# Averaging 8,192 rows in windows of 16: each partition owns 64 neighbouring rows, and the output stays on chip until the last load

## The chip, the cores and the metric

The kernel runs on one core of a Trainium2 chip. The metric is device time in microseconds (us), taken as the median of several runs; less is better. A timed run is the whole program. A separately profiled execution gives the trace that the views below come from, and its span (first to last instruction) is a little shorter than a timed run.

## What is computed

The input `x` is float32 of shape (32, 256, 4096) and `output_size` is 256. Length 4096 splits evenly, so every output is the mean of 16 neighbouring values:

```python
for i in range(output_size):
    start = int(i * length / output_size)
    end = int((i + 1) * length / output_size)
    result[:, :, i] = np.mean(x[:, :, start:end], axis=-1)
```

Batch and channel are only a list of 8,192 rows of 4096 values (16 KB each). A core reads 134.2 MB, writes 8.4 MB, and does one addition per value read.

## The kernel before, in words

**Tiling.** The 8,192 rows are cut into 16 tiles of 512 rows, 8.4 MB each. A tile is a contiguous piece of DRAM: partition p of tile t holds the R = 4 rows 512t + 4p to 512t + 4p + 3. So a partition's share of a tile is 64 KB without a gap, and the shares of neighbouring partitions are 64 KB apart in DRAM (`x3`). In the output the same four rows are 4 KB, and neighbouring partitions are 4 KB apart (`out3`).

**Buffers.** `inpool` has two input tiles `xin` of 64 KB per partition; `foldpool` two fold buffers of 8 KB; `accpool` three sums of 4 KB; `outpool` three results of 4 KB; `defer_buf` holds four tiles' results (16 KB) until the end. A tile framework puts in the semaphore waits: load t + 2 goes into the buffer of tile t, so its issue on the queue of SyncE (SP) waits until the readers of tile t are done.

**One steady tile** (`steady_plan`). One load of 8.4 MB on the SP queue (line 152). Of the tile's 1,024 windows, VectorE (DVE) sums the first 512 directly over 16 values (`vdir`, line 168). For the other 512, GpSimd (POOL) first adds the two halves of each window, 8 + 8 values, into a fold buffer, in two pieces of 256 windows (`fold`, line 161); VectorE then sums the remaining 8 values (`vfold`, line 177). ScalarE (ACT) multiplies by 1/16 (`mulA`, line 184) and issues the tile's store of 512 KB on its own queue (`store`, line 200).

**Exceptions.** The first two tiles' loads are each split over the SP and ACT queues (`ramp`). Tiles 9 to 12 (`DEFER`) aren't stored when done: their results wait in `defer_buf`. Tiles 13 and 14 (`two_chunk_plan`) are loaded in two halves. The last tile (`last_plan`) is loaded in six pieces, from 4,096 KB down to 256 KB; behind them in the SP queue stands one store of the four deferred tiles (`dstore_all`, line 194, 2,048 KB); its results go out in two stores of 896 and 128 columns, each split over both queues (lines 206 and 209).

**What sets the order.** Each engine and each queue works in program order. Transfers that one queue has issued are worked off one after another by the core's 16 DMA engines; transfers of the SP and the ACT queue share these engines. There is no planner.

Of the kernel before, what the change touches and what calls it, by code (L numbers as in the profile page):

```python
# [9 lines left out]
def kernel(  # L10
# [5 lines left out]
):  # L16
    nc = tc.nc

# [5 lines left out]
    hw = window // 2  # L24

    rows = batch * channels
    P = nc.NUM_PARTITIONS

    R = 4
    IN_BUFS = 2  # L30
    RAMP_TILES = 2

    assert rows % (P * R) == 0
    ntiles = rows // (P * R)

    x3 = x.rearrange("b c l -> (b c) l").rearrange(
        "(t p r) l -> t p (r l)", p=P, r=R
    )
    out3 = out.rearrange("b c o -> (b c) o").rearrange(
        "(t p r) o -> t p (r o)", p=P, r=R  # L40
    )

    inv_w = 1.0 / float(window)
    groups = R * output_size
    cols = R * length
    half_g = groups // 2
    quarter_g = groups // 4
    FOLD_CAP = 256
    DEFER_N = 4
    DEFER_T0 = ntiles - 3 - DEFER_N  # L50
    DEFER = set(range(DEFER_T0, DEFER_T0 + DEFER_N))

    out_def = out.rearrange("b c o -> (b c) o").rearrange(
        "(t p r) o -> p t (r o)", p=P, r=R
    )

    inpool = ctx.enter_context(tc.tile_pool(name="inpool", bufs=IN_BUFS))
    foldpool = ctx.enter_context(tc.tile_pool(name="foldpool", bufs=2))
    accpool = ctx.enter_context(tc.tile_pool(name="accpool", bufs=3))
    OUT_BUFS = 3  # L60
    outpool = ctx.enter_context(tc.tile_pool(name="outpool", bufs=OUT_BUFS))
    deferpool = ctx.enter_context(tc.tile_pool(name="deferpool", bufs=1))
    defer_buf = deferpool.tile([P, DEFER_N * groups], mybir.dt.float32)
    defer3 = defer_buf.rearrange("p (t o) -> p t o", t=DEFER_N, o=groups)

    def steady_plan(i, ramp=False):
        ops = []
        if ramp:
            ops.append(("load", 0, cols // 2, "sync"))
            ops.append(("load", cols // 2, cols, "scalar"))  # L70
        else:
            ops.append(("load", 0, cols, "sync"))
        ops += [
            ("fold", half_g, half_g + quarter_g),
            ("fold", half_g + quarter_g, groups),
            ("vdir", 0, half_g),
            ("vfold", half_g, half_g + quarter_g),
            ("vfold", half_g + quarter_g, groups),
            ("mulA", 0, groups),
        ]  # L80
        if i not in DEFER:
            ops.append(("store", 0, groups))
        return ops

    def two_chunk_plan(i):
        h = cols // 2
        ops = [
            ("load", 0, h, "sync"),
            ("load", h, cols, "sync"),
        ]  # L90
        for c in range(2):
            g0 = c * half_g
            ops.append(("fold", g0 + 192, g0 + 352))
            ops.append(("fold", g0 + 352, g0 + 512))
            ops.append(("vdir", g0, g0 + 192))
            ops.append(("vfold", g0 + 192, g0 + 352))
            ops.append(("vfold", g0 + 352, g0 + 512))
        ops += [
            ("mulA", 0, groups),
            ("store", 0, groups),  # L100
        ]
        return ops

    def last_plan(i):
        sizes = [256, 256, 192, 128, 64, 64, 32, 32]
        assert sum(sizes) == groups
        bounds = [0]
        for s in sizes:
            bounds.append(bounds[-1] + s)
        ops = []  # L110
        load_bounds = [0, 512, 832, 896, 960, 992, 1024]
        for k in range(len(load_bounds) - 1):
            g0, g1 = load_bounds[k], load_bounds[k + 1]
            ops.append(("load", g0 * window, g1 * window, "sync"))
        ops.append(("dstore_all",))
        part1 = 896
        for k, s in enumerate(sizes):
            g0, g1 = bounds[k], bounds[k + 1]
            if s >= 128:
                m = (g0 + g1) // 2  # L120
                ops.append(("fold", m, g1))
                ops.append(("vdir", g0, m))
                ops.append(("vfold", m, g1))
            else:
                ops.append(("vdir", g0, g1))
            if g1 == part1:
                ops.append(("mulA", 0, part1))
                ops.append(("store2", 0, part1))
        ops.append(("mulV", part1, groups))
        ops.append(("store2", part1, groups))  # L130
        return ops

    def plan_for(i):
        if i < RAMP_TILES:
            return steady_plan(i, ramp=True)
        idx_from_end = ntiles - 1 - i
        if idx_from_end == 0:
            return last_plan(i)
        if idx_from_end <= 2:
            return two_chunk_plan(i)  # L140
        return steady_plan(i)

    def emit(i, ops, bufs):
        xin, xin_2d, acc, res = bufs
        fold_tiles = {}

        for op in ops:
            kind = op[0]
            if kind == "load":
                _, c0, c1, qname = op  # L150
                q = nc.sync if qname == "sync" else nc.scalar
                q.dma_start(out=xin_2d[:, c0:c1], in_=x3[i][:, c0:c1])  # L152
            elif kind == "fold":
                _, g0, g1 = op
                n = g1 - g0
                assert n <= FOLD_CAP
                ftile = foldpool.tile(
                    [P, FOLD_CAP, hw], mybir.dt.float32, name="foldt"
                )
                fold_tiles[(g0, g1)] = ftile  # L160
                nc.gpsimd.tensor_add(  # L161
                    out=ftile[:, 0:n, :],
                    in0=xin[:, g0:g1, 0:hw],
                    in1=xin[:, g0:g1, hw:window],
                )
            elif kind == "vdir":
                _, g0, g1 = op
                nc.vector.reduce_sum(  # L168
                    out=acc[:, g0:g1],
                    in_=xin[:, g0:g1, :],  # L170
                    axis=mybir.AxisListType.X,
                )
            elif kind == "vfold":
                _, g0, g1 = op
                ftile = fold_tiles[(g0, g1)]
                n = g1 - g0
                nc.vector.reduce_sum(  # L177
                    out=acc[:, g0:g1],
                    in_=ftile[:, 0:n, :],
                    axis=mybir.AxisListType.X,  # L180
                )
            elif kind == "mulA":
                _, g0, g1 = op
                nc.scalar.mul(out=res[:, g0:g1], in_=acc[:, g0:g1], mul=inv_w)  # L184
            elif kind == "mulV":
                _, g0, g1 = op
                nc.vector.tensor_single_scalar(  # L187
                    out=res[:, g0:g1],
                    in_=acc[:, g0:g1],
                    scalar=inv_w,  # L190
                    op=mybir.AluOpType.mult,
                )
            elif kind == "dstore_all":
                nc.sync.dma_start(
                    out=out_def[:, DEFER_T0 : DEFER_T0 + DEFER_N, :],
                    in_=defer3[:, 0:DEFER_N, :],
                )
            elif kind == "store":
                _, g0, g1 = op
                nc.scalar.dma_start(  # L200
                    out=out3[i][:, g0:g1], in_=res[:, g0:g1]
                )
            elif kind == "store2":
                _, g0, g1 = op
                h = P // 2
                nc.scalar.dma_start(
                    out=out3[i][h:P, g0:g1], in_=res[h:P, g0:g1]
                )
                nc.sync.dma_start(
                    out=out3[i][0:h, g0:g1], in_=res[0:h, g0:g1]  # L210
                )
            else:
                raise AssertionError(kind)

    res_by_tile = {}

    def new_bufs(i):
        xin = inpool.tile([P, groups, window], mybir.dt.float32)
        xin_2d = xin.rearrange("p o w -> p (o w)")
        acc = accpool.tile([P, groups], mybir.dt.float32)  # L220
        if i in DEFER:
            j = i - DEFER_T0
            res = defer_buf[:, j * groups : (j + 1) * groups]
        else:
            res = outpool.tile([P, groups], mybir.dt.float32)
        res_by_tile[i] = res
        return xin, xin_2d, acc, res

    ramp_bufs = []
# [49 lines left out]
```

## Time and profile before

| | |
|---|---|
| Timed runs (3) | 337.47 us median (337.29 to 337.67) |
| Span of the profiled execution | 335.2 us |
| Part of a timed run outside the span | 337.47 - 335.2 = 2.3 us |
| VectorE busy | 209.5 us (62%) in 64 instructions |
| GpSimd busy | 145.6 us (43%) in 42 instructions |
| ScalarE busy | 18.1 us (5%) in 17 instructions |
| DMA | 142.62 MB in 6033 packets, mean 425 GB/s over the span |

The profiled execution has no separate time of its own beside its span, so the row "outside the span" sets the span against the median of the timed runs.

How to read the views: the page gives each engine's busy time as a digit (tenths) in 40 equal slices of the span, and below that the mean busy share of the 16 DMA engines and the GB/s they moved. The chain of waits follows the work that ended last backwards to what released it. The timeline lists instructions in order, with the idle time before each and what ended it. The table of windows gives busy time per engine, DMA share and GB/s for stretches of the span. The trace also has a record of every single DMA packet with its size and duration; a packet is one contiguous run between DRAM and one partition, moved by one of the 16 engines.

### The profile page before, as it was taken

How to read it: one execution, taken by the hardware profiler on the slowest of the kernel's cores; microseconds unless marked ns; L12 is line 12 of the kernel's file. 1: busy time of each engine (PE TensorE's matmuls, PEld its weight loads, DVE VectorE, ACT ScalarE, POOL GpSimd, SP SyncE). 2: the span in 40 equal slices, each digit the busy share in tenths (PEclk: the TensorE clock that was granted, in tenths of full speed). 3: DMA queues.
4: the chain of work that ended last, by engine and by line, in shares of the span. 5: the costliest groups of instructions: out<-in, count | busy, mean ns of one | idle time of the engine just before them, and what ended most of it. 6: DMA issues, size and time to landing. Idle time of an engine off the chain costs nothing.

```text
span 335.2 us, 279 instructions
## 1 busy us (share of the span) xinstructions
DVE 209.5 (62%) x64; ACT 18.1 (5%) x17; POOL 145.6 (43%) x42
## 2 busy tenths in 40 slices
DVE  0029295590956919478293773928659299765595
ACT  1000101001010000101001010010100101000101
POOL 0027091550906419063280723708154276664460
DMA  8999999999999999999999999999898999999997
GB/s 317 434 438 438 501 399 399 475 456 399 399 476 455 399 399 493 438 399 399 516 414 399 399 532 399 399 400 507 375 501 375 438 438 438 438 396 458 404 410 273
DMA packets 6033, 142.62 MB, mean 425 GB/s; under 512 B 656, under 2 KB 784, under 8 KB 3344
## 3 DMA queue, kind: packets, MB, share of 16 engines
q1 hardware_dynamic: 4000, 128.19, 89.0%
q10 hardware_dynamic: 2032, 14.42, 10.2%
q14 instruction: 1, 0.01, 0.0%
HBM read 134.22 MB, written 8.39 MB: 425 GB/s over the span
## 4 chain that ended last, share of the span: by engine, by line
DMA 78%; POOL 18%; DVE 2%; issue 0%; SPq 0%; ACTq 0%; POOLq 0%
DMA xin<-in_x_dram 78%; POOL foldt L161 18%; DVE acc L168 1%; DVE acc L177 0%; SPq L152 0%; ACTq L152 0%; DVE res L187 0%; POOLq L161 0%
## 5 line engine op out<-in xcount | busy, mean ns | idle before, releaser
L161 POOL TENSOR_TENSOR foldt<-xin 128x2048 f32<-128x2048 f32 (+4 forms) x38 | 145.4, 3848 | 180.4 <-DMA xin<-in_x_dram 178.4
L168 DVE TENSOR_REDUCE acc<-xin 128x512 f32<-128x8192 f32 (+5 forms) x25 | 137.4, 5504 | 118.6 <-DMA xin<-in_x_dram 118.6
L177 DVE TENSOR_REDUCE acc<-foldt 128x256 f32<-128x2048 f32 (+4 forms) x38 | 73.9, 1976 | 3.3 <-POOL foldt L161 3.1
L184 ACT ACTIVATE res<-acc 128x1024 f32<-128x1024 f32 (+1 forms) x12 | 12.6, 1047 | 234.6 <-DVE acc L177 220.4
L184 ACT ACTIVATE defer_buf<-acc 128x1024 f32<-128x1024 f32 x4 | 4.2, 1056 | 75.6 <-DVE acc L177 75.6
L184 ACT ACT_TABLE_LOAD x1 | 1.3, 1283 | 1.7 <-PEq L260 1.7
L187 DVE TENSOR_SCALAR res<-acc 128x128 f32<-128x128 f32 x1 | 0.2, 226 | 0.0
L260 POOL MEMSET const-float32-0.0<- 128x1 f32 x1 | 0.1, 98 | 0.2 <-issue 0.2
L260 POOL MEMSET const-bfloat16-1.0<- 128x1 bf16 x1 | 0.1, 102 | 0.0
L260 POOL MEMSET const-uint8-127<- 128x1 uint8 x1 | 0.1, 102 | 0.0
L260 POOL MEMSET const-float32-1.0<- 128x1 f32 x1 | 0.1, 98 | 0.0
## 6 DMA issues: line engine op xcount, KB each, us to landing
xin<-in_x_dram SPq DMA_DIRECT2D x7, 4096.0 KB, 25.3
xin<-in_x_dram ACTq DMA_DIRECT2D x2, 4096.0 KB, 31.6
out_dram<-res ACTq DMA_DIRECT2D x11, 512.0 KB, 27.0
xin<-in_x_dram SPq DMA_DIRECT2D x1, 2560.0 KB, 31.8
out_dram<-defer_buf SPq DMA_DIRECT2D x1, 2048.0 KB, 22.9
xin<-in_x_dram SPq DMA_DIRECT2D x2, 512.0 KB, 33.4
xin<-in_x_dram SPq DMA_DIRECT2D x2, 256.0 KB, 25.1
out_dram<-res SPq DMA_DIRECT2D x1, 224.0 KB, 3.0
```

The costliest lines, as they stand in the source:

```text
L161: nc.gpsimd.tensor_add(out=ftile[:, 0:n, :], in0=xin[:, g0:g1, 0:hw], in1=xin[:, g0:g1, hw:window],)
L168: nc.vector.reduce_sum(out=acc[:, g0:g1], in_=xin[:, g0:g1, :], axis=mybir.AxisListType.X,)
L177: nc.vector.reduce_sum(out=acc[:, g0:g1], in_=ftile[:, 0:n, :], axis=mybir.AxisListType.X,)
L184: nc.scalar.mul(out=res[:, g0:g1], in_=acc[:, g0:g1], mul=inv_w)
L187: nc.vector.tensor_single_scalar(out=res[:, g0:g1], in_=acc[:, g0:g1], scalar=inv_w, op=mybir.AluOpType.mult,)
L260: nc = _bacc.Bacc("TRN2", target_bir_lowering=False, num_devices=1)
```

## The change

The same 16 steps of 8.4 MB, but a partition now owns 64 neighbouring rows of the 8,192 (1 MB of input, 64 KB of output), and step t takes rows 4t to 4t + 3 of each partition's 64. A partition's share of a load is still 64 KB without a gap; the shares of neighbouring partitions are now 1 MB apart in DRAM. All loads are single DMAs on the SP queue. POOL folds half of the windows in place, in one instruction, and VectorE reads the folded half out of the input tile. VectorE writes straight into `res`, which holds the whole output (64 KB per partition), and ScalarE scales it in place. One store of tiles 0 to 14 (60 KB per partition, 7.9 MB) is issued on the SP queue right behind the last load; the last tile's 512 KB go out on the ACT queue.

The plans, the ramp, the deferred store and the fold, sum and result buffers are gone. The core of the diff, with the removed functions cut (they stand in the listing above):

```diff
-    x3 = x.rearrange("b c l -> (b c) l").rearrange(
-        "(t p r) l -> t p (r l)", p=P, r=R
-    )
-    out3 = out.rearrange("b c o -> (b c) o").rearrange(
-        "(t p r) o -> t p (r o)", p=P, r=R
-    )
...
+    ROWS = rows // P
+    ntiles = ROWS // R
+    cells = R * output_size
+    m = cells // 2
+    xp = x.rearrange("b c l -> (b c) l").rearrange("(p r) l -> p (r l)", p=P, r=ROWS)
+    op = out.rearrange("b c o -> (b c) o").rearrange("(p r) o -> p (r o)", p=P, r=ROWS)
+
+    inpool = ctx.enter_context(tc.tile_pool(name="inpool", bufs=2))
+    respool = ctx.enter_context(tc.tile_pool(name="respool", bufs=1))
+    res = respool.tile([P, ntiles * cells], F32, name="res")
+    held = (ntiles - 1) * cells
...
-    def steady_plan(i, ramp=False):
...
-    def two_chunk_plan(i):
...
-    def last_plan(i):
...
-    def emit(i, ops, bufs):
...
+    for t in range(ntiles):
+        xin = inpool.tile([P, cells, window], F32, name="xin")
+        base = t * cells
+        nc.sync.dma_start(
+            out=xin.rearrange("p o w -> p (o w)"),
+            in_=xp[:, base * window : (base + cells) * window],
+        )
+        if t == ntiles - 1:
+            nc.sync.dma_start(out=op[:, 0:held], in_=res[:, 0:held])
+        nc.gpsimd.tensor_add(
+            out=xin[:, m:cells, 0:hw],
+            in0=xin[:, m:cells, 0:hw],
+            in1=xin[:, m:cells, hw:window],
+        )
+        nc.vector.reduce_sum(
+            out=res[:, base : base + m], in_=xin[:, 0:m, :], axis=X
+        )
+        nc.vector.reduce_sum(
+            out=res[:, base + m : base + cells], in_=xin[:, m:cells, 0:hw], axis=X
+        )
+        nc.scalar.mul(
+            out=res[:, base : base + cells],
+            in_=res[:, base : base + cells],
+            mul=inv_w,
+        )
+    nc.scalar.dma_start(out=op[:, held:], in_=res[:, held:])
```

More of the change, by code (lines that the diff above doesn't have):

```diff
@@ L4 @@
 import concourse.tile as tile
-from concourse import bass_utils, mybir
+from concourse import mybir
 from concourse._compat import with_exitstack
@@ L17 @@
     nc = tc.nc
+    F32 = mybir.dt.float32
+    X = mybir.AxisListType.X
     batch, channels, length = x.shape
@@ L24 @@
     hw = window // 2
-    rows = batch * channels
+    inv_w = 1.0 / float(window)
     P = nc.NUM_PARTITIONS
     R = 4
-    IN_BUFS = 2
-    RAMP_TILES = 2
+    rows = batch * channels
     assert rows % (P * R) == 0
-    ntiles = rows // (P * R)
-    x3 = x.rearrange("b c l -> (b c) l").rearrange(
-        "(t p r) l -> t p (r l)", p=P, r=R
-    )
-    out3 = out.rearrange("b c o -> (b c) o").rearrange(
-        "(t p r) o -> t p (r o)", p=P, r=R
-    )
-    inv_w = 1.0 / float(window)
-    groups = R * output_size
@@ L45 @@
[L45 to L64, printed above, removed]
-    def steady_plan(i, ramp=False):
[L67 to L83, printed above, removed]
@@ L85, in two_chunk_plan @@
-    def two_chunk_plan(i):
[L86 to L102, printed above, removed]
@@ L104, in last_plan @@
-    def last_plan(i):
[L105 to L141, printed above, removed]
-    def emit(i, ops, bufs):
[L144 to L229, printed above, removed]
@@ L230 @@
-    for i in range(RAMP_TILES):
-        bufs = new_bufs(i)
-        ops = plan_for(i)
-        loads = [op for op in ops if op[0] == "load"]
-        emit(i, loads, bufs)
-        ramp_bufs.append(
-            (i, [op for op in ops if op[0] != "load"], bufs)
-        )
-    for i, ops, bufs in ramp_bufs:
-        emit(i, ops, bufs)
-    for i in range(RAMP_TILES, ntiles):
-        bufs = new_bufs(i)
-        emit(i, plan_for(i), bufs)
+    ROWS = rows // P
+    ntiles = ROWS // R
+    cells = R * output_size
```

## The prediction

> **What bounds the kernel now.** I read the page's 40 slices first. The DMA row stands at 9 from the second slice to the last but one, while VectorE and POOL have gaps in every tile:
>
> ```profile
> DVE  0029295590956919478293773928659299765595
> ...
> POOL 0027091550906419063280723708154276664460
> DMA  8999999999999999999999999999898999999997
> ```
>
> Then the table of windows (DMA share and GB/s are the last two columns) says how full "9" is:
>
> ```profile
> 0.00:1.50 1.50, 0.00 (x0) 0.00 (x0) 0.20 (x4) 1.00 0.00 0
> 1.50:3.00 1.50, 0.00 (x0) 1.28 (x1) 0.00 (x0) 1.00 1.28 350
> 3.00:310.00 307.00, 192.13 (x50) 14.79 (x14) 135.75 (x34) 1.00 1.00 433
> 310.00:330.00 20.00, 15.93 (x13) 2.01 (x2) 9.68 (x5) 1.00 0.99 412
> 330.00:332.00 2.00, 1.45 (x4) 0.00 (x0) 0.00 (x0) 1.00 1.01 316
> 332.00:333.50 1.50, 0.00 (x0) 0.00 (x0) 0.00 (x0) 1.00 0.68 218
> 333.50:335.20 1.70, 0.00 (x0) 0.00 (x0) 0.00 (x0) 1.00 0.00 0
> ```
>
> For 307 us the DMA engines never rest (1.00) and move 433 GB/s; VectorE works 192 of them, POOL 136. The last 5 us carry less, and the first and last 1.7 us nothing. The chain of waits puts 18% on POOL:
>
> ```profile
> DMA 78%; POOL 18%; DVE 2%; issue 0%; SPq 0%; ACTq 0%; POOLq 0%
> ```
>
> That is no POOL bound. The timeline of one steady tile shows why:
>
> ```profile
> 83.33 8.69 DVE L168 TENSOR_REDUCE acc<-xin 128x512 f32<-128x8192 f32 x1 [7.56 <-DMA xin<-in_x_dram]
> 83.36 8.86 POOL L161 TENSOR_TENSOR foldt<-xin 128x2048 f32<-128x2048 f32 x2 [11.70 <-DMA xin<-in_x_dram]
> 91.93 4.47 DVE L177 TENSOR_REDUCE acc<-foldt 128x256 f32<-128x2048 f32 x2
> 92.25 0.33 SPq L152 DMA_DIRECT2D xin<-in_x_dram  x1
> 96.43 1.06 ACT L184 ACTIVATE res<-acc 128x1024 f32<-128x1024 f32 x1 [19.58 <-DVE acc L177]
> 97.52 0.34 ACTq L200 DMA_DIRECT2D out_dram<-res  x1
> 103.86 8.69 DVE L168 TENSOR_REDUCE acc<-xin 128x512 f32<-128x8192 f32 x1 [7.46 <-DMA xin<-in_x_dram]
> ```
>
> The buffer is free at 92.25, and its next load is issued, 11.6 us before the load already in flight lands (103.86). So the time is the sum of the DMA packets, and I price the change in packets. The trace's packet records, grouped by size (DMA time = count x mean / 16 engines):
>
> ```
> bytes  count  mean ns  max ns  us/16   what
> 65536   1408   2419     2568   212.9   loads
> 32768   1152   1224     2295    88.1   loads (ramp, half tiles); median 1213
> 20480    128    763      771     6.1   load
>  4096   2176    159      174    21.6   1920 stores (19.1), 256 loads (2.5)
>  3584    128    216      413     1.7   last store, first part
>  2048    256     86       96     1.4   loads
>   512    128     28       44     0.2   last store, second part
>     4    656      9       12     0.4   semaphore writes
> ```
>
> Sum 332.5 us. The first packet starts at 1.7 us, the last ends at 333.4: 331.65 us, a little under the sum, because packets of two queues overlap at both ends. So the span of 335.2 is 1.7 + 331.65 + 1.8.
>
> **The change, part by part.** (1) *Packets.* All loads become 2,048 packets of 64 KB: 2048 x 2419 / 16 = 309.7 us. The first packets of the 32 KB ramp took some 1.9 us for 1.2, so I add 0.7 once: 310.4. The held store is 128 packets of 61,440 bytes. No such write is in the trace; 4,096-byte packets show no difference between 1,920 writes and 256 reads (159 ns, at most 174), so I take the line between the two large reads: 2418 - 4096 x (2418 - 1213) / 32768 = 2267 ns, times 8 per engine, 18.1 us. The last store is 8 x 159 = 1.3 us, semaphore writes about 0.2. Sum 330.0 us against 331.65: **1.65 us less**. The writes give most of it (21.0 to 19.4), the loads the rest (311.1 to 310.4).
>
> (2) *One queue, no ramp, whole tiles.* The first load is issued at the same point (0.7 us). The ramp only divided the same bytes over two queues. VectorE starts later, but it isn't the bound. I cost it at nothing beyond the 0.7 above.
>
> (3) *Fold in place, buffer held longer.* Now the buffer is free only when VectorE has read the folded half: 8.86 + 4.47 = 13.3 us after landing instead of 8.9. Add 0.3 for the issue and 1.0 to the first packet (0.74 to 1.7 at the start): 14.7, against 8 x 2.419 = 19.35 us that the other buffer's load takes. Cover 4.6 us. Two loads are issued ahead as before, so SP has no bubble. POOL's output moves from a packed tile to runs of 8 values in 16, which no row shows. The nearest row, the same addition on the same input runs, gives 8.86 us for 512 windows; I take that (no loss). At the other end, I count a strided write as dear as one of the two strided inputs, 8.86 / 2 = 4.43 us more: an estimate from that row. That would use up the 4.6 us just so. A gain below nothing is hidden by the loads.
>
> (4) *The end.* SP's last instruction is the held store. It waits for tile 14's scaling, 8.86 + 4.47 + 1.06 = 14.4 us after that tile's landing, and is issued before the last load ends (19.35); nothing stands behind it on SP. So it starts without a gap when the last load lands, and for 18.1 us covers the last tile's compute: 14.5 us with small gaps, then 1.5 from issue to first packet as in the last store of before, 16.0. Cover 2.1 us; then 1.3 us of last store. Without cover (POOL at +4.43) the end comes 4.43 - 2.1 = 2.3 us later. VectorE's 32 instructions instead of 64, and ACT's 12 stores fewer, lie beside the transfers: nothing.
>
> (5) *The pitch.* At any moment the 16 engines read 16 partitions' shares, so far 64 KB (and multiples) apart, now 1 MB. No row of before reads at that pitch. The steady packets show no strain: 2418 ns is the median, 43 of 1408 take over 2430, so a gain is excluded to within a few ns each. The nearest row for a loss is the slowest of the 1408, 2568 ns; if every packet took so long, 128 x 149 ns = 19.0 us more. I take nothing, because the typical packet is nearer to that, and keep 19.0 for the range.
>
> Against this speaks a rule of the Trainium skill, "DMA: Bandwidth & Descriptors", section "Latency and other measured facts". It reports that copies of 128-partition tiles between HBM tensors slow down when the rows lie a large power of two apart: 207 GB/s at 512 KiB and 164 at 2 MiB, against 214 undisturbed; its explanation is marked an inference. By its 512 KiB figure the loads would take 309.7 x 214 / 207 = 320 us and the kernel about 346 us; by its 2 MiB figure 404 and 430 us. It was measured with 16 KiB pieces, reads and writes mixed; the trace of before has no pitch to test it.
>
> **The rivals.** *A, forecast:* packets at their old pace, 335.2 - 1.65 = 333.55 us of span; with the 2.27 us outside the span, 337.47 - 1.65 = **335.8 us**. Chance 0.52. For: packets of the same size for 300 us at one duration, and cover at each wait. Against: the unseen pitch.
>
> *B, the 1 MB pitch slows the reads:* in every load, all 128 packets per engine. It decides from 1.65 us / 128 = 13 ns a packet (0.5%) and is measurably slower from 18 ns. At half the bound, 75 ns, 335.8 + 9.6 = 345.4; at the bound 354.8 us. For: no load has ever run at this pitch, and each packet's nanosecond is multiplied by 128. Against: no packet of before is short of bandwidth. Chance 0.32.
>
> *C, POOL in place is slow:* decides at the end from +2.1 us per fold, in every tile from +4.6. At +4.43, 335.8 + 2.3 = 338.1 us. Against: the input runs of before were strided already. Chance 0.08, half of it within 0.2%.
>
> *D, it gains nothing that shows:* 8 to 18 ns more per packet pay back the gain, 336.8 to 338.1 us. Chance 0.08.
>
> **How the numbers follow.** 0.2% is 0.7 us, about what a measurement of this kernel can tell from no change. Faster: A, 0.52. Within 0.2%: D and half of C, 0.12. Slower: B and half of C, 0.36. The forecast's own range is 334.3 to 336.8: its low end drops the 0.7 at the start and compares sum with sum (332.5 - 329.3 = 3.2 us less). The whole range takes in the pitch bound and C: 335.8 + 19.0 + 2.3 = 357. About 0.15 lies outside, nearly all above.
>
> **What would show it.** Right: 2,048 packets of 65,536 bytes at 2.42 us, DMA share 1.00 and some 433 GB/s to the end of the loads at 312 us, then 18 us in which the held store alone moves data, the last tile's scaling done before it ends, one short store, span 333.5. POOL L58 at 8.9 us each shows step 3. Wrong: packets longer than 2.43 us with GB/s under 433 in the load windows (B); a hole in the DMA row between the held store and the last store, or SP issuing a load after the load before it has landed (C). A held store that takes other than 18 us breaks the estimate of step 1.

## The result, and the profile after

The changed kernel is slower: 356.84 us median (350.73 to 364.3, 6 runs) against 337.54 us (337.29 to 337.67, 6 runs). The ratio is 1.0442, 95% interval 1.0414 to 1.0469; it rests on the two lowest runs (354.09 and 350.73), because a comparison leaves out runs far above the fastest, and with the two medians it would be 1.057. The scatter is news in itself: the kernel before varied by 0.4 us, this one by 13.6. The profiled run took 354.09 us, its span is 352.3.

The page of after, its DMA row and the GB/s row beneath:

```profile
DMA  8999999999999999999999999999999999998994
GB/s 283 424 342 365 379 350 402 424 409 424 439 394 424 424 357 417 424 439 439 402 439 417 446 365 432 402 446 409 439 424 424 461 365 394 439 446 387 455 446 192
```

The DMA row looks as good as before: the engines are busy. But busy is not the same as moving bytes. The windows of after (busy time of VectorE, ScalarE, POOL; then TensorE clock, DMA share, GB/s):

```profile
2.00:331.00 329.00, 196.58 (x30) 15.86 (x16) 130.76 (x15) 1.00 1.00 410
331.00:350.00 19.00, 13.11 (x2) 1.06 (x1) 8.72 (x1) 1.00 0.89 383
350.00:352.30 2.30, 0.00 (x0) 0.00 (x0) 0.00 (x0) 1.00 0.08 32
```

The share is 1.00 while the loads run, as it was, at 410 GB/s where there were 433. So the average packet takes longer. The packet records say which (p90: nine in ten are no longer):

```
after      count  mean ns  median   p90   max   us/16   forecast
65536       2048     2548    2418  2856  4329   326.2   310.4
61440        128     2267    2267  2267  2267    18.1    18.1
 4096        128      160     159   162   169     1.3     1.3
semaphores   288        9       9     9     9     0.2     0.2
```

Half of the load packets still take 2418 ns or so; a good third (742 of 2,048) take over 2430, up to 4329. The two stores are within 0.05 us of their forecast. The chain of waits names POOL and VectorE, as it named POOL before, and is as little a proof here:

```profile
DMA 67%; POOL 17%; DVE 10%; POOLq 3%; issue 0%; ACT 0%; SPq 0%
```

The end, in the timeline:

```profile
326.94 0.35 SPq L57 DMA_DIRECT2D out_dram<-res  x1
332.11 8.69 DVE L63 TENSOR_REDUCE res<-xin 128x512 f32<-128x8192 f32 x1 [6.29 <-DMA xin<-in_x_dram]
332.22 8.72 POOL L58 TENSOR_TENSOR xin<-xin 128x4096 f32<-128x4096 f32 x1 [10.85 <-DMA xin<-in_x_dram]
340.97 4.42 DVE L66 TENSOR_REDUCE res<-xin 128x512 f32<-128x4096 f32 x1 [0.17 <-POOL xin L58]
345.43 1.06 ACT L69 ACTIVATE res<-res 128x1024 f32<-128x1024 f32 x1 [18.52 <-DVE res L66]
346.51 0.37 ACTq L74 DMA_DIRECT2D out_dram<-res  x1
```

The held store is issued 5 us before the last load lands, and the last tile's compute (14.4 us) runs beside it, as planned. VectorE, POOL and ScalarE do nothing late.

### The profile page after: what moved, and what is told of

The parts are those of the page before. It is cut to its first block, busy times and chain, and to the rows that moved or that the text cites. A ratio compares the mean times of both kernels' runs of the same rounds, so it can differ in the third digit from the quotient of the medians.

```text
span 352.3 us, 159 instructions
## 1 busy us (share of the span) xinstructions
DVE 209.7 (60%) x32; ACT 18.2 (5%) x17; POOL 139.7 (40%) x20
## 4 chain that ended last, share of the span: by engine, by line
DMA 67%; POOL 17%; DVE 10%; POOLq 3%; issue 0%; ACT 0%; SPq 0%
DMA xin<-in_x_dram 67%; POOL xin L58 17%; DVE res L66 10%; POOLq L105 2%; ACT res L69 0%; SPq L52 0%; POOLq L58 0%
## 5 line engine op out<-in xcount | busy, mean ns | idle before, releaser
L58 POOL TENSOR_TENSOR xin<-xin 128x4096 f32<-128x4096 f32 x16 | 139.5, 8717 | 201.0 <-DMA xin<-in_x_dram 201.0
L63 DVE TENSOR_REDUCE res<-xin 128x512 f32<-128x8192 f32 x16 | 139.0, 8686 | 133.0 <-DMA xin<-in_x_dram 133.0
L66 DVE TENSOR_REDUCE res<-xin 128x512 f32<-128x4096 f32 x16 | 70.7, 4420 | 2.7 <-POOL xin L58 2.5
L69 ACT ACTIVATE res<-res 128x1024 f32<-128x1024 f32 x16 | 16.9, 1056 | 327.6 <-DVE res L66 327.6
```

The lines of the kernel that those rows point to most:

```text
L58: nc.gpsimd.tensor_add(out=xin[:, m:cells, 0:hw], in0=xin[:, m:cells, 0:hw], in1=xin[:, m:cells, hw:window],)
L63: nc.vector.reduce_sum(out=res[:, base : base + m], in_=xin[:, 0:m, :], axis=X)
L66: nc.vector.reduce_sum(out=res[:, base + m : base + cells], in_=xin[:, m:cells, 0:hw], axis=X)
L69: nc.scalar.mul(out=res[:, base : base + cells], in_=res[:, base : base + cells], mul=inv_w,)
```

## The experiments

Theory P: the spacing of exactly 1 MB between the partitions' shares makes the load packets longer. Rival Q: something else in the new program does. Rival S: it is the distance, not the exact spacing. Later: L, the loss needs engines that read at the same place of their packets at the same time; N, it doesn't.

**1. The new program with the old row order** (`e1_old_rows`).

```diff
-    xp = x.rearrange("b c l -> (b c) l").rearrange("(p r) l -> p (r l)", p=P, r=ROWS)
-    op = out.rearrange("b c o -> (b c) o").rearrange("(p r) o -> p (r o)", p=P, r=ROWS)
+    x3 = x.rearrange("b c l -> (b c) l").rearrange("(t p r) l -> t p (r l)", p=P, r=R)
+    o3 = out.rearrange("b c o -> (b c) o").rearrange("(t p r) o -> p t (r o)", p=P, r=R)
...
-            in_=xp[:, base * window : (base + cells) * window],
+            in_=x3[t],
```

> The program of after (whole loads on one queue, fold in place, output held until the last load) with the row order of before: shares of neighbouring partitions 64 KB apart in DRAM, and the held store in pieces of 4 KB. Theory P (the 1 MB spacing makes the load packets longer): all 64 KB packets back at 2419 ns; loads 310.4 us, held store 1920 x 159 / 16 = 19.1, last store 1.3, so 336.7 us, and the GB/s row flat at 433. Rival Q (something in the new program does it: the buffers held longer, or engines disturbing the loads by the in-place fold): packets stay near 2548 ns on average and the time near 354.

Measured: 335.75 us (335.53 to 335.82), ratio 0.9951 [0.9936, 0.9966]. The 64 KB packets average 2429 ns; the DMA times sum to 331.5 us. One window of its steady part has the old pace:

```profile
40.00:310.00 270.00, 183.48 (x28) 14.78 (x14) 122.05 (x14) 1.00 1.00 432
```

Q falls: everything else in the change, taken together and with the held store in pieces of 4 KB, makes the kernel 1.65 us faster than the kernel before, which took 337.40 us beside it. It is 1 us under the expectation; where that microsecond lies is told below.

**2. The old program with the new row order** (`e2_new_rows_old_program`).

```diff
-        "(t p r) l -> t p (r l)", p=P, r=R
+        "(p t r) l -> t p (r l)", p=P, r=R
...
-        "(t p r) o -> t p (r o)", p=P, r=R
+        "(p t r) o -> t p (r o)", p=P, r=R
```

and the same for the deferred store (`out_def`).

> The program of before with one thing changed, the row order: a partition owns 64 neighbouring rows, so shares are 1 MB apart. Theory P: 64 KB packets at about 2550 ns on average instead of 2419, the 32 KB packets longer by a like part; 130 ns x 88 plus 70 ns x 72 per engine is some 16 us, so 345 to 362 us, and the time differs by several us between runs. Rival Q: 337.5 us within 0.7.

Measured: 357.7 us (354.4 to 373.33), ratio 1.0599 [1.0578, 1.062]. The row order alone carries the whole loss, and the scatter with it. 64 KB packets average 2490 ns (2550 expected), 32 KB packets 1329 (before: 1224). The edit moves the stores' rows too, but these don't make the loss: in after the loads are slow from the first one on, and no store starts before the last load is nearly through (328.4 us). The GB/s row shows most of the loss in the first eight slices (70 us), where the ramp and the first whole loads run:

```profile
GB/s 257 331 365 361 361 374 371 379 419 395 435 411 458 403 451 395 418 428 449 428 442 411 458 419 428 418 420 446 417 461 409 409 439 431 428 428 438 418 403 177
```

**3. Spacing of 960 KB** (`e3_pitch_960k`). A partition owns 60 rows of the first 7,680; the last load takes the other 512 rows as before.

```diff
+    n1 = P * (ROWS - R)
+    xp = xr[0:n1, :].rearrange("(p r) l -> p (r l)", p=P, r=ROWS - R)
+    op = orr[0:n1, :].rearrange("(p r) o -> p (r o)", p=P, r=ROWS - R)
+    xl = xr[n1:rows, :].rearrange("(p r) l -> p (r l)", p=P, r=R)
+    ol = orr[n1:rows, :].rearrange("(p r) o -> p (r o)", p=P, r=R)
...
-            in_=xp[:, base * window : (base + cells) * window],
+            in_=xl if t == ntiles - 1 else xp[:, base * window : (base + cells) * window],
...
-            nc.sync.dma_start(out=op[:, 0:held], in_=res[:, 0:held])
+            nc.sync.dma_start(out=op, in_=res[:, 0:held])
...
-    nc.scalar.dma_start(out=op[:, held:], in_=res[:, held:])
+    nc.scalar.dma_start(out=ol, in_=res[:, held:])
```

> The program of after, but a partition owns 60 neighbouring rows of the first 7,680 (shares 960 KB apart, no power of two) and 4 of the last 512 (64 KB apart, read by the last load). Packets have the same sizes as in after. Theory P in its narrow form (it is the power of two that hurts): 64 KB packets at 2419 ns, 335.8 us as first forecast for after. Rival S (it is the distance: 128 places spread over all 134 MB instead of one stretch of 8 MB): packets as long as in after, about 350 to 360 us.

Measured: 334.93 us (334.85 to 335.09), ratio 0.9928 [0.9914, 0.9943]: **faster than both kernels**, by 0.7% against the kernel before, and the best of this study; 0.9 us under the expectation. Rival S falls; the rows lie almost as far apart as in after. Its windows:

```profile
2.00:312.00 310.00, 196.58 (x30) 15.86 (x16) 130.76 (x15) 1.00 1.00 432
312.00:330.00 18.00, 13.11 (x2) 1.06 (x1) 8.72 (x1) 1.00 0.96 417
330.00:333.10 3.10, 0.00 (x0) 0.00 (x0) 0.00 (x0) 1.00 0.42 168
```

Set against after's windows: the busy times of the three engines are the same to 0.1 us, the DMA share while the loads run is the same, and the GB/s and the length differ. This is the kernel that the forecast described: packets 2426 ns, loads over at 312, 18 us of held store, last packet at 331.76.

**4. Spacing of 512 KB** (`g2_pitch_512k`): the rows in two halves, 32 rows of each to a partition.

```diff
-    xp = x.rearrange("b c l -> (b c) l").rearrange("(p r) l -> p (r l)", p=P, r=ROWS)
+    xp = x.rearrange("b c l -> (b c) l").rearrange("(g p r) l -> g p (r l)", g=G, p=P)
...
+            nc.sync.dma_start(out=op[:, 0 : G - 1, :], in_=resg[:, 0 : G - 1, :])
+            nc.sync.dma_start(out=op[:, G - 1, 0 : gc - cells], in_=resg[:, G - 1, 0 : gc - cells])
```

> The program of after with the rows in two halves: a partition owns 32 neighbouring rows of each half, shares 512 KB apart; held store in two DMAs of 32 KB and 28 KB per partition. Theory P expects a loss that shrinks with the spacing: between none and half of after's 17 us, 336 to 345 us. Rival S expects the 67 MB spread to cost nearly as much as 134 MB: over 348.

Measured: 335.47 us (335.38 to 335.73), ratio 0.9945 [0.993, 0.996], packets 2427 ns. No loss at all; I had thought of a slope, and there is an edge between 512 KB and 1 MB. The time lies half a microsecond under the expected 336 to 345.

**5 to 8. How far from 1 MB is far enough?** A partition owns a few windows less than 16,384; the rest (a few windows per partition) is loaded and stored apart at the start.

```diff
-    cells = R * output_size
+    cells = 1020
+    rem = ROWS * output_size - ntiles * cells
...
+    n1 = P * ntiles * cells
+    xp = xf[0 : n1 * window].rearrange("(p f) -> p f", p=P)
+    xe = xf[n1 * window :].rearrange("(p f) -> p f", p=P)
```

1,020 windows in a tile give 1 MB minus 4 KB, 1,023 give minus 1 KB. For minus 256 and minus 64 bytes only the last tile is shorter, by 4 windows and by 1.

> The program of after with tiles of 1,020 windows instead of 1,024, so that shares lie 1 MB minus 4 KB apart (16 tiles), and the 64 windows per partition left over come in one small load and store at the start. Theory P1 (what hurts is that the 16 streams keep the same low address bits; a shift of 4 KB per partition is enough to undo it): packets of 65,280 bytes at 2.41 us, about 335.5 us, like the 960 KB spacing. Theory P2 (only the high address bits count: spacings near 1 MB are all bad, 960 KB was far enough off): packets of 2.5 us or more, 348 to 364 us.

> The same with tiles of 1,023 windows: shares 1 MB minus 1 KB apart, 16 windows per partition left over. P1 gives the size of the shift that is needed: 335 to 337 us if 1 KB is enough, 345 to 364 if not. P2: 348 to 364 us.

> The program of after with a partition owning 4 windows less (16,380), so that shares lie 1 MB minus 256 bytes apart; the last tile is 4 windows shorter, and 4 windows per partition are loaded and stored apart at the start. Spacings of 1 MB minus 4 KB and minus 1 KB ran at full pace. If the streams must differ by about 1 KB or more per partition, this one is slow again, 345 to 364 us with 64 KB packets over 2500 ns; if any departure from the exact 1 MB will do, 335 to 337 us.

> The same with one window less: 1 MB minus 64 bytes. Expected slower than with 256 bytes or the same: as after (350 to 364 us) if the size of the shift counts, 335 to 337 us if only exact multiples of 1 MB hurt.

Measured, with the other spacings beside them (load packets of 64 KB or nearly; means of one profiled run; the kernel before had medians of 337.33 to 337.54 us beside them):

```
spacing          us median (range)          mean ns   max ns
64 KB  (e1)      335.75 (335.53 to 335.82)     2429     3591
512 KB           335.47 (335.38 to 335.73)     2427     3367
960 KB           334.93 (334.85 to 335.09)     2426     3613
1 MB - 4 KB      335.38 (335.16 to 335.69)     2416     3469
1 MB - 1 KB      335.50 (335.42 to 335.91)     2425     3669
1 MB - 256 B     340.66 (340.37 to 341.27)     2460     4053
1 MB - 64 B      360.44 (359.36 to 364.74)     2654     6951
1 MB   (after)   356.84 (350.73 to 364.3)      2548     4329
```

One KB less per partition ends the loss; 64 bytes don't help; 256 bytes help most of the way. So P2 falls, and the edge that P1 asked for lies between 64 bytes and 1 KB. P1's reason, equal low address bits, isn't shown by this: shares 512 KB apart agree in their low 19 address bits, and they lost nothing. The longest packets say little by themselves, since the undisturbed kernels have some of 3.4 to 3.7 us too. The first windows of four kernels show it without any packet record. After:

```profile
2.00:60.00 58.00, 22.89 (x4) 1.07 (x2) 17.44 (x2) 1.00 0.99 372
60.00:120.00 60.00, 37.61 (x6) 3.17 (x3) 25.40 (x3) 1.00 1.00 419
```

Minus 64 bytes, minus 256 bytes, minus 1 KB:

```profile
2.00:60.00 58.00, 13.09 (x3) 1.71 (x3) 8.72 (x1) 1.00 0.97 292
60.00:120.00 60.00, 39.31 (x6) 3.17 (x3) 26.15 (x3) 1.00 1.00 401
```

```profile
2.00:60.00 58.00, 26.25 (x5) 2.19 (x4) 17.43 (x2) 1.00 0.99 397
60.00:120.00 60.00, 39.32 (x6) 3.74 (x4) 26.15 (x3) 1.00 1.00 434
```

```profile
2.00:60.00 58.00, 26.43 (x5) 2.77 (x4) 17.41 (x2) 1.00 0.99 423
60.00:120.00 60.00, 39.34 (x7) 3.17 (x3) 26.10 (x3) 1.00 1.01 436
```

From 2 to 60 us the last column goes 372, 292, 397, 423 at DMA shares of 0.97 to 0.99. In the slow kernels the loss is worst at the start and shrinks later: with 256 bytes to nothing that shows (430 to 436 GB/s from 60 us on), but in after it stays at 414 to 419 GB/s up to 300 us.

**9 and 10. Staggering the engines, first try** (`s_stagger`, `s_control`): 14 extra small loads at the start, over 15 to 2 partitions, and the control over 16 each. These and the next two load the extra pieces on top of the whole computation.

```diff
+    for j in range(14):
+        n = 15 - j
+        c0 = (2 + j) * cells
+        nc.scalar.dma_start(out=res[0:n, c0 : c0 + cells], in_=xp[0:n, 0:cells])
```

> After with its 1 MB spacing, and at the start 14 extra small loads on the ACT queue, of 15, 14, ... 2 partitions and 4 KB each (into parts of the output buffer that are overwritten later), meant to give the first DMA engines more to do than the last, so that the engines no longer stand at the same place of their 64 KB packets. Theory L (the loss comes from engines marching in step): the 64 KB packets average well under 2500 ns from the first tiles on, 338 to 346 us. Rival N (step doesn't matter, the addresses alone do): packets as in after, 2550 ns, 352 to 366 us.

> The control for the staggering: the same 14 extra loads, each over 16 partitions, so that every engine gets the same extra work (14 packets of 159 ns, 2.2 us). Both theories: the time of after plus 2 us, 352 to 366 us. If this one is fast too, it is the disturbance at the start and not the stagger that matters.

Measured: 363.56 us (361.12 to 366.49) and 369.5 us (365.7 to 372.63). The times say little, since I put in a wait that I had not meant: SP waited 30.7 us for an extra load before it issued the second tile's load. The two share no buffer, so I take it for a semaphore that both use; that isn't shown. DMA fell to 137 GB/s in the fourth slice. The packets average 2587 and 2589 ns, and the control lies above its expected 352 to 366. Inconclusive; the next pair avoids the wait.

**11 and 12. Staggering, second try** (`s_stagger6`, `s_control6`).

```diff
+    for j, n in enumerate([15, 12, 10, 8, 6, 3]):
+        c0 = (2 + 2 * j) * cells
+        nc.scalar.dma_start(out=res[0:n, c0 : c0 + 2 * cells], in_=xp[0:n, 0 : 2 * cells])
```

The control has `[16] * 6` in place of the list.

> The staggering once more, with six extra loads of 8 KB per partition over 15, 12, 10, 8, 6 and 3 partitions, which leaves semaphores free so that no load of a tile waits for them. Theory L (1 MB spacing hurts because engines stand at the same place of their packets): 64 KB packets average under 2600 ns in the first 60 us, where after has some 2820, and the whole takes 338 to 348 us. Rival N: 2750 ns or more in the first 60 us, 350 to 366 us.

> Its control: the same six extra loads, each over 16 partitions, so that no engine is put ahead. Both theories: as after plus the extra packets (6 x 0.3 = 1.9 us), 352 to 366 us, and first packets of 2750 ns or more.

Measured: 349.01 us (348.21 to 349.41), ratio 1.0339 [1.0323, 1.0355], against 358.85 us (354.08 to 362.37), 1.0523 [1.0486, 1.056], for the control. These are 9.8 us between the medians, and 6.1 between the staggered kernel and the control's two lowest runs (354.08 and 356.13), on which its ratio rests. The 54 extra packets instead of 96 explain 42 x 0.31 / 16 = 0.8 us of it, or 1.6 with the times that these packets took in the two traces (1.4 and 3.0 us per engine). First the staggered kernel, then its control:

```profile
2.00:60.00 58.00, 22.08 (x4) 2.34 (x2) 17.44 (x2) 1.00 0.99 382
60.00:120.00 60.00, 40.91 (x7) 3.17 (x3) 26.16 (x3) 1.00 1.01 436
```

```profile
2.00:60.00 58.00, 19.15 (x3) 2.34 (x2) 14.72 (x2) 1.00 0.99 351
60.00:120.00 60.00, 37.99 (x7) 3.17 (x3) 24.77 (x4) 1.00 1.01 422
```

So unequal extra work for the engines at the start takes away part of the loss, with the tile loads at the same addresses; and the staggered kernel's runs scatter by 1.2 us, its control's by 8.3. Nearly all of the gain lies in the first 120 us. Behind that the two kernels' windows of 60 us are much alike: 423, 429 and 424 GB/s against 422, 421 and 426. That it comes from engines standing at different places of their packets is not shown: the first 128 load packets, in groups of 16 in a row, start within 0.8 to 2.2 us in the one and within 0.9 to 1.8 in the other. Both forecasts for the staggered kernel miss: packets of the first 60 us average 2712 ns (control 2932, as expected), between L's 2600 and N's 2750, and 349 lies above L's 348 and below N's 350.

## Why the prediction was wrong

**The step that failed is (5), the pitch.** It said "I take nothing, because the typical packet is nearer to that", and put rival B at 0.32. In the profiled run the loads came to 326.2 us of packet time instead of 310.4: 15.8 us. A further 3.6 us come from engines that idle: the packets sum to 345.8 us per engine, but run from 1.75 to 351.1 us, 349.4. More than half of that idle time lies at the end, where the 16 engines finish the held store between 346.7 and 349.9 us, out of pace; at the 960 KB spacing they finish within 0.6 us. The forecast had no term for this. With 0.6 us less at the end, the span is 15.8 + 3.6 - 0.6 = 18.8 us over the 333.55 forecast. The sign was wrong because a row of one spacing was taken to speak for another: 1,408 packets at 64 KB spacing said nothing of 1 MB, as the text itself stated. That left the choice between the ends open, and the typical packet was no ground for it.

**B's bound.** 2568 ns for every packet was built on the slowest packet before. The mean of after is 2548, close to it by luck: single packets took 4329, the idle engines were not in the bound, and the slowest run took 364.3. At 1 MB minus 64 bytes the mean was 2654, above the bound. The median of 356.84 lies just inside the range's 357, but on the other side of the kernel before than forecast.

**The rule that spoke against it.** The Trainium skill, "DMA: Bandwidth & Descriptors", section "Latency and other measured facts", had pointed the right way: rows a large power of two apart slow the copies, and at 4 MiB a pad of 4 KiB restores the rate while one of 192 bytes does not. Here, at 1 MB, a shift of 4 KB or 1 KB restores it, 64 bytes don't, and 256 do mostly: the same kind of edge. Its figure of 207 out of 214 GB/s at 512 KiB is not seen for these reads, which lose nothing there (335.47 us); and the prediction's estimate from that figure, 346 us, was too little for 1 MB (356.84).

**Steps that held**, seen best in the 960 KB kernel, where step (5) has no part:

- (1) packets: 330.0 us forecast, 330.03 measured from first to last packet (1.73 to 331.76). The held store's 2267 ns, drawn as a line between two sizes, was met exactly. The 0.7 us at the start is there too: packets of the first 20 us average 2506 ns, later ones 2421, 8 x 85 ns.
- (2) one queue and no ramp: nothing, as said.
- (3) fold in place: 8.72 us in one instruction against 8.86 in two. Runs of 8 in 16 on the output cost POOL nothing, and rival C has no part in the loss.
- (4) the end: last store issued 14.4 us after landing, held store 18.1 us. The cover held.
- The 960 KB kernel is still 0.9 us under the 335.8 forecast: 0.5 us after the last packet (1.3 instead of 1.8) and 0.5 outside the span (334.85 - 333.1 = 1.75 instead of 2.27). Of the latter, 0.27 was a slip: the forecast set the span of one execution against the median of others, and in all 21 later runs of the kernel before the part outside is 2.0 us (337.48 - 335.5, for one). The rest differs between the programs: 2.0 us in both that have 279 instructions, 1.7 to 1.8 in the others (159 to 186). Why is not shown. The first experiment's missing microsecond is the same.

**What stays open.** That the spacing of 1 MB is the cause is shown in both directions (experiments 1 and 2) and by the shifts. Why it slows the reads stays open. A disturbance at the start that is unequal between the engines matters (11 and 12). Yet it is not simply that engines in step are slow: in the kernel of 1 MB minus 1 KB, the load packets, in groups of 16 in a row, start within 0.6 to 0.7 us and all is well, while in after a group spreads over 1.1 to 1.9 us at first and typically 2.3 later. Nor does the spread make packets slow: in the kernel of minus 256 bytes it is some 2.3 us too, and from 60 to 300 us its packets average 2418 to 2422 ns. Where in the memory the reads hinder each other, if they do, and why 512 KB is free and 1 MB is not, no run here tells.

## What to carry to other kernels

A DMA share of 1.00 says that the engines are occupied, not how fast they move bytes (433 GB/s before, 410 after): set GB/s and the time of one packet beside it. Before a change of layout, write down the DRAM distance between neighbouring partitions; if it becomes a large power of two that no row has shown, that is the first risk to price, and a cheap one to avoid (60 rows instead of 64, or 1 KB less, cost nothing here). And a price taken at one spacing is no bound at another (2568 ns here, against a mean of 2654 at 1 MB minus 64 bytes).

## What the runs showed of the hardware that was not expected

Reads 512 KB apart ran at 2427 ns per 64 KB packet and reads 1 MB apart at 2548, with single packets up to 4329 (3367 at 512 KB); 64 bytes off 1 MB gave 2654 and 6951, 1 KB off gave 2425 and 3669. The loss is worst in the first 60 us: 372 GB/s against 423 with 1 KB off, then 414 to 419 against 428 to 436 up to 300 us. About half of it falls into that first stretch (8.4 of 16.7 us per engine that the load packets took beyond 2418 ns each). It makes runs of the same program differ by 13.6 us where those of the undisturbed kernels differ by 0.2 to 0.6.
